# Two sets of projection tiles in plain fp32 instead of split products, and the scan's pace set by a count of the tiles' demands

## Chip, cores and metric

The kernel runs on 1 core of one Trainium2 chip. The metric is device time in microseconds from the start to the end of one execution. Before the change the median of 3 runs is 3599.55 us (3596.58 to 3600.33).

## What is computed

One sequence of 256 tokens of width 2048 runs through two blocks in fp32. The first (attention, a state-space branch and a large expert layer) isn't touched. The second, cut to what matters:

```python
h = rms_norm_2(x, norm_w[i])
proj = h @ w_in[i]
(g_qkv, g_z, g_b, g_a, r_feat, r_z, s_u, s_z, gate_logits) = _split_cols(proj, SPLIT_SIZES)
o_a = gdn_branch(g_qkv, g_z, g_b, g_a, ...)
o_b = rwkv7_branch(r_feat, r_z, ...)
o_c = s5_branch(s_u, s_z, ...)
gates = sigmoid(gate_logits + gate_b)          # 3 x 2048 columns
merged = sum(gates * einsum('blnc,ncd->blnd', stack([o_a, o_b, o_c]), w_branch), branch)
x = x + merged @ w_out
return rms_norm_2(x, final_norm_w)
```

S5 (`s5_branch`) is a complex diagonal recurrence over time on `s_u` (1024 channels, 32 groups of 128 states in the kernel). The recurrent branch (`rwkv7_branch`) takes keys and two small low-rank inputs out of `r_feat`.

## The kernel before, in words

**Tiles of weights.** Every projection streams weight tiles of 128 x 1024 fp32 (512 KB). The normal way (`wt`, L287) is in three terms: SyncE loads the tile into a `raw` buffer (L267, four buffers), ScalarE copies it to a reduced-precision high half `whi` (L281), VectorE subtracts to get the low half `wlo` (L285), and TensorE makes high x high, high x low and low x high (`mm3`, L298; lines 300 to 302). There are two `whi`/`wlo` pairs in the staging pool and a third in the second block (`self.third`), taken in turn. The other way (`whole`, L290) loads a tile straight into one of these `whi`/`wlo` buffers, seen as plain fp32, and needs no split; only the first block's output projection uses it (`tm_whole`, L1378, matmul at L1387, two times four groups of four tiles).

**Two shapes of projection.** `cm` (L1338) puts the weights' columns on the partitions: two tiles for 128 output columns, 8 contraction steps a tile, each of three products with 256 moving columns (L300 to L302), or two products (`mm2`, L304) where it is given room. `tm` (L1361) puts tokens on the partitions: eight tiles for 512 output columns, a tile having 2 contraction steps for each of 2 token halves, three products of 512 columns. Both are generators: a step loads and splits a tile (`yield`) and the next step issues its matmuls.

**The order of the work.** `feed` puts generators in one queue and `fill` (L1412) takes one step of the first. The second block's code calls `fill` between the instructions of its serial parts, so tiles lie between them. The tile framework then orders each engine's instructions by when they can run, with the order of the code as the priority; each engine works its own queue in order at run time.

**The second block's start.** `x2_stage` (L1289) ends the first block: it forms `x2` and `x1`, the norm's factors (L1311 to L1318), then `h3` (L1326) turns the normed state into `hT`, high and low halves of 16 chunks of 128 x 256: two TensorE turns a chunk (L443), a ScalarE copy (L453) and a VectorE subtraction (L455), both out of PSUM. Then VectorE rescales `x2` (L1322) and ScalarE's queue stores it to DRAM (`x3d`, L1323) for the residual. `block2` (L1464) allocates its pools over memory that `x1` and `x2` held. It feeds S5's inputs (`w2s`, 8 times `cm`, evacuated by `evu`), with the first three groups of gates after inputs 1, 2 and 3, then the keys (`w2rk`, 10 times `cm`, fed by `rwkv_front`, L1871, evacuated by `evk`), then four more gate groups; `gates` holds 12 groups in all. So 16 + 20 tiles of `cm` and 56 of `tm` lie in the queue when S5 starts.

**S5** (L1715) has 8 groups `j` of 4 state steps `i`. A group loads its tables (L1739, L1746), turns its input matrix (L1742) and copies it (L1744). A state step loads a cosine and sine table (L1751), TensorE makes the inputs (L1758, for two states at a time), VectorE multiplies twice (L1764, L1765), GpSimd combines (L1766, L1767), VectorE scans twice (L1770), GpSimd and VectorE multiply (L1771, L1772) and VectorE combines (L1773, L1774). `back` (L1729 to L1733) turns four states into outputs. After each state step `self.fill(3 if sc % 4 else 2)` takes 2 or 3 tiles from the queue. `self.until(("u", j))` takes tiles until input `j` is there.

`merged` (128 x 2 x 2048) collects the three branches, first written in the evacuation of `branch(2, ...)` long after S5.

Of the kernel before, what the change touches and what calls it, by code (L numbers as in the profile page):

```python
# [12 lines left out]
ALU = mybir.AluOpType  # L13
# [220 lines left out]
class K:  # L234
    def __init__(self, tc, A, at, dbg=None):
        self.tc, self.nc, self.A, self.at, self.dbg_ = tc, tc.nc, A, at, dbg
        self.n = 0
        self.pp, self.queue, self.done, self.bg = [], [], set(), []
        self.bgr, self.bgc = 1.0, 0.0
        self.side, self.later = [], [[] for _ in range(LAG)]  # L240
        self.nw = 0
        self.third, self.ns = None, 0
        self.more, self.nr = None, 0

    def t(self, pool, shape, dt=F32, tag=None, bufs=None):
        self.n += 1
# [23 lines left out]
    def split(self, src, n=1024, hi_e="act", lo_e="dve"):  # L270
        self.ns = (self.ns + 1) % 3
        p, tag, b = (self.third, "3", 1) if self.third and self.ns == 0 else (self.stg, "", 2)
        hi = self.t(p, [128, 1024], F32R, tag="whi" + tag, bufs=b)
        lo = self.t(p, [128, 1024], F32R, tag="wlo" + tag, bufs=b)
        self.hilo(hi[:, :n], lo[:, :n], src[:, :n], hi_e, lo_e)
        return hi, lo

    def hilo(self, hi, lo, src, hi_e="act", lo_e="dve"):
# [11 lines left out]
    def whole(self, src):  # L290

        self.nw = (self.nw + 1) % (6 if self.third else 4)
        p, n = (self.third, "3") if self.nw > 3 else (self.stg, "")
        t = self.t(p, [128, 1024], F32R, tag=("whi", "wlo")[self.nw % 2] + n, bufs=1 if n else 2).bitcast(F32)
        self.nc.sync.dma_start(t, src)
        return t

    def mm3(self, out, shi, slo, mhi, mlo, start, stop):  # L298
# [990 lines left out]
    def x2_stage(self, hp, xp, out, x1, nf, g2):  # L1289

        nc, tc = self.nc, self.tc
        V, ACT, PL = nc.vector, nc.scalar, nc.gpsimd
        scr = tc.alloc_tile_pool(name="scr2", bufs=1, space=DRAM)
        x3d = self.t(scr, [2, 128, D], tag="x3d")
        x2 = self.t(xp, [128, 2, D])
        ss = self.t(xp, [128, 2, 2, 4])
        for b in range(4):
            c = slice(b * 512, b * 512 + 512)
            for q in range(2):
                x, y = x2[:, q, c], x1[:, q, c]  # L1300
                V.tensor_tensor(x, out[4 * q + b], g2[:, c], op=ALU.mult)
                (PL if q and b < 2 else V).tensor_tensor(x, x, y, op=ALU.add)
                junk = self.t(xp, [128, 512], tag="junk", bufs=2)
                ACT.activation(junk, x, AF.Square, accum_out=ss[:, 0, q, b : b + 1])
                (V if q or b == 3 else PL).tensor_tensor(y, x, nf[:, c], op=ALU.mult)
                junk = self.t(xp, [128, 512], tag="junk", bufs=2)
# [12 lines left out]
        hT = self.h3(hp, xp, x1, v)  # L1319
        for q in range(2):  # L1320
            for c in (slice(0, 1024), slice(1024, 2048)):
                V.tensor_scalar(x2[:, q, c], x1[:, q, c], r[:, q : q + 1], None, op0=ALU.mult)  # L1322
            nc.scalar.dma_start(x3d[q], x2[:, q])  # L1323
        return hp, hT, x3d

    def h3(self, hp, pool, y, r):  # L1326

        hT = self.pair(hp, NK, "hh")
        hh, hl = hT[:2]
        dg = self.diag(pool, r, "dg3", 2)  # L1330
        n2 = self.cp("norm2", "cp3")
        for c in range(16):
            a = [y[:, q, c * 128 : c * 128 + 128] for q in range(2)]
            self.chunk_T(a, [dg[:, q] for q in range(2)], hh[:, c], hl[:, c], n2[:, c : c + 1], c % 2)
        return hT


    def cm(self, wd, j, hT, evac, key=None, nk=NK, room=None):  # L1338


        ps = self.t(self.acc, [128, 512], tag="acc")
        for half in range(2):
            hi, lo = self.wt(wd[2 * j + half], nk // 2 * 128)
            yield
            for k in range(nk // 2):
                kk = half * (nk // 2) + k
                sl = slice(k * 128, k * 128 + 128)
                if room:
                    self.mm2(ps, hi[:, sl], lo[:, sl], hT[2][:, kk], kk == 0, kk == nk - 1)
                else:  # L1350
                    self.mm3(ps[:, :S], hi[:, sl], lo[:, sl], hT[0][:, kk], hT[1][:, kk], kk == 0, kk == nk - 1)
        if room:
            s = room()
            self.nc.scalar.activation(s, ps[:, S:], AF.Copy)
            self.nc.vector.tensor_tensor(s, ps[:, :S], s, op=ALU.add)  # L1355
            evac(j, s)
        else:
            evac(j, ps[:, :S])
        self.done.add(key)

    def tm(self, wd, g, hT, evac, key=None, nk=NK):  # L1361
# [99 lines left out]
        self.flush()  # L1461


    def block2(self, hp, hT, x3d):  # L1464

        nc, tc, A = self.nc, self.tc, self.A
        V, ACT, PL = nc.vector, nc.scalar, nc.gpsimd
# [10 lines left out]
        merged = self.t(gt, [128, 2, D])  # L1478

        def gate(g):  # L1480
            def ev(g, q, ps):
# [10 lines left out]
        def branch(n, g4, o, last=None):  # L1492
            def ev(g, q, ps):
                c = slice(g4 * 512, g4 * 512 + 512)
                th = self.t(gt, [128, 512], tag="th", bufs=2)
                nc.sync.dma_start(th, gd[g, q])
                if n == 2:
                    V.scalar_tensor_tensor(merged[:, q, c], th, 1.0, ps, op0=ALU.add, op1=ALU.mult)
                else:
                    V.scalar_tensor_tensor(th, th, 1.0, ps, op0=ALU.add, op1=ALU.mult)  # L1500
                    (PL if last is None else V).tensor_tensor(merged[:, q, c], merged[:, q, c], th, op=ALU.add)
# [11 lines left out]
            ACT.activation(u[:, j], ps, AF.Copy)  # L1513

        gates = [gate(g) for g in (8, 9, 10, 11, 4, 5, 6, 7, 0, 1, 2, 3)]
        for j in range(8):
            self.feed(self.cm(A["w2s"], j, hT, evu, ("u", j)))
            if j in (1, 2, 3):
                self.feed(gates.pop(0))
        yT = out2("B")  # L1520
        kT = mB()
        self.rwkv_front(br, hT, kT)
        self.feed(*gates[:4])
        del gates[:4]
        self.s5(br, u, yT)
        oS = out2("A")
        gk, gq, gvz = self.gdn_front(br, hT)
# [17 lines left out]
        def last(g4):  # L1545
            for c in range(4 * g4, 4 * g4 + 4):
                ps = self.bank()
                for q in range(2):
                    nc.tensor.transpose(ps[:, q * 128 : q * 128 + 128], merged[:, q, c * 128 : c * 128 + 128], self.ident)
# [6 lines left out]
        self.dbg("merged", merged)  # L1556
        self.third = None
        gt.release()
        br.release()
        with tc.tile_pool(name="fin", bufs=1) as fp:  # L1560
            y = self.t(fp, [128, 2, D])
            fw = self.t(fp, [128, D])
# [152 lines left out]
    def s5(self, pl, u_, yT):  # L1715
# [7 lines left out]
        def back(j, u, cT, states):  # L1723
# [8 lines left out]
            ACT.activation(y, y, AF.Gelu_apprx_tanh)  # L1732
            self.hilo(yh[:, j], yl[:, j], y)  # L1733

        for j in range(8):
            self.until(("u", j))
            u = u_[:, j]
# [10 lines left out]
            for i in range(4):  # L1748
# [26 lines left out]
                states.append(a)  # L1775
                if late and i == 0:
                    late()
                self.fill(3 if sc % 4 else 2)
            late = partial(back, j, u, cT, states)
        late()  # L1780

# [86 lines left out]
            yield  # L1868


    def rwkv_front(self, pl, hT, kT):  # L1871
        nc, A = self.nc, self.A
        V, ACT, PL, mm = nc.vector, nc.scalar, nc.gpsimd, nc.tensor.matmul
        cp = lambda n: self.cp(n, "cp3")
# [44 lines left out]
                    nc.tensor.transpose(pt[:, q * 128 : q * 128 + 128], t[:, q * 128 : q * 128 + 128], self.ident)  # L1919
                V.tensor_copy(self.ba, pt[:, 0:256].rearrange("p (q c) -> p q c", q=2)[:, :, 96:112])  # L1920

        for j in range(10):
            self.feed(self.cm(A["w2rk"], j, hT, evk, ("rk", j)))
        self.rw = dict(shift=shift, wa=wa, half=half, oka=oka, ones=ones, hln=hln, pss=pss, kT=kT)

    def rwkv(self, pl, hT, out, extras):

# [360 lines left out]
    def run(self, upto=99, only=0):  # L2288
# [4 lines left out]
        if only == 2:  # L2293
# [7 lines left out]
            with tc.tile_pool(name="x3p", bufs=1) as p:  # L2301
# [6 lines left out]
                hT = self.h3(hp, p, x3, self.rstd(p, ss, 2, float(D)))  # L2308
            self.block2(hp, hT, x3d)
        else:  # L2310
            r = self.block1(upto)
            if r is not None:
# [26 lines left out]
```

## Time and profile before

| | |
|---|---|
| median of 3 runs | 3599.55 us |
| the profiled execution | 3600.31 us |
| its span, first to last instruction | 3598.2 us |
| mean granted TensorE clock | 0.979 |
| VectorE busy / ScalarE busy / GpSimd busy | 71% / 45% / 11% |

The profile is one execution, taken by the hardware profiler. Busy times are per engine. Matmuls are pipelined and their ends are modelled, so the busy time of a run of matmuls is not what they cost; the distance between starts is. PE is TensorE's matmuls, PEld its weight loads, DVE VectorE, ACT ScalarE, POOL GpSimd, SP SyncE. A granted clock of 1.00 is 2.4 GHz, 0.50 is 1.2 GHz.

### The profile page before, as it was taken

The page shows a single profiled execution, that of the slowest core. Times are in us where ns is not written, and L with a number is a line of the kernel's source. Part 1 is how long each engine was busy: PE and PEld are TensorE (multiplying, and loading weights), DVE is VectorE, ACT ScalarE, POOL GpSimd, SP SyncE. Part 2 cuts the span into 40 slices and gives each one's busy share as a digit, 9 for nine tenths or more (in the row PEclk, how much of TensorE's full clock was granted, in tenths as well). Part 3 has the DMA queues.
Part 4 walks back from the last instruction along what each step waited for, and adds up shares of the span by engine and source line. Part 5 has one row for each costly group of instructions (what it writes and reads, how often), then busy time and mean ns, then how long its engine had stood idle before and what let it go on. Part 6 is the DMA issues. An engine that isn't in the chain of part 4 may idle for free. (4 is left out here: it accounts for less than half of the span.)

```text
span 3598.2 us, 52389 instructions
## 1 busy us (share of the span) xinstructions
PE 3427.4 (95%) x18918; PEld 2852.2 (79%) x18918; DVE 2565.5 (71%) x4648; ACT 1632.8 (45%) x2934; POOL 390.3 (11%) x487
## 2 busy tenths in 40 slices
PE   5899999999999999999999998988999999999998
PEld 4888747888998888888878786776788888778887
DVE  7777666788887655565577658878777767666765
ACT  2355424444554444445555554333444444434444
POOL 0000010000000000000000002333223222021310
PEclk7999999999999999999999999999999999999999
DMA  9966785666456855566788765645533443434455
GB/s 345 333 222 206 266 290 177 199 198 201 159 162 208 257 185 186 187 203 205 240 271 287 254 206 186 203 160 180 169 113 113 150 138 108 134 123 159 146 182 186
DMA packets 237294, 710.40 MB, mean 197 GB/s; under 512 B 34091, under 2 KB 61804, under 8 KB 235756
## 3 DMA queue, kind: packets, MB, share of 16 engines
q1 hardware_dynamic: 207564, 672.08, 56.8%
q10 hardware_dynamic: 29472, 34.98, 2.9%
q8 instruction: 149, 2.44, 0.3%
q14 instruction: 109, 0.89, 0.1%
HBM read 673.87 MB, written 32.55 MB: 196 GB/s over the span
## 5 line engine op out<-in xcount | busy, mean ns | idle before, releaser
L285 DVE TENSOR_TENSOR wlo<-raw,whi 128x1024 fp32r<-128x1024 f32 (+1 forms) x951 | 1167.8, 1229 | 567.1 <-ACT whi L281 562.8
L281 ACT ACTIVATE whi<-raw 128x1024 fp32r<-128x1024 f32 (+1 forms) x951 | 994.0, 1046 | 1224.8 <-PE acc L302 577.3
L308 PE MATMUL acc<-hh,whi 128*128 128x512 f32 x3328 | 1197.9, 401 | 0.7 <-DVE cT L469 0.7
L309 PE MATMUL acc<-hh,wlo 128*128 128x256 f32 x3328 | 940.0, 282 | 7.1 <-DVE wlo L285 6.9
L308 PEld LDWEIGHTS acc<-hh,whi 128*128 128x128 f32 x3328 | 627.0, 188 | 145.6 <-issue 4.5
L309 PEld LDWEIGHTS acc<-hh,wlo 128*128 128x128 f32 x3328 | 629.6, 189 | 13.5 <-DVE wlo L285 12.0
L301 PE MATMUL acc<-wlo,wh 128*128 128x512 f32 x1024 | 402.1, 393 | 8.0 <-DVE wlo L285 7.2
L300 PE MATMUL acc<-whi,wh 128*128 128x512 f32 x1024 | 396.6, 390 | 3.5 <-DVE ge L1355 2.8
L302 PE MATMUL acc<-whi,wl 128*128 128x512 f32 x1024 | 399.3, 390 | 0.0
L301 PE MATMUL acc<-wlo,hh 128*128 128x512 f32 (+1 forms) x608 | 243.7, 401 | 14.9 <-DVE wlo L285 14.7
L300 PE MATMUL acc<-whi,hh 128*128 128x512 f32 (+1 forms) x608 | 248.1, 409 | 5.3 <-DVE r L1355 5.3
L302 PE MATMUL acc<-whi,hh 128*128 128x512 f32 (+1 forms) x608 | 242.1, 398 | 0.0
L301 PEld LDWEIGHTS acc<-wlo,wh 128*128 128x128 f32 x1024 | 192.5, 188 | 58.6 <-DVE wlo L285 18.8
L300 PEld LDWEIGHTS acc<-whi,wh 128*128 128x128 f32 x1024 | 192.3, 188 | 45.7 <-ACT wh L281 3.1
L302 PEld LDWEIGHTS acc<-whi,wl 128*128 128x128 f32 x1024 | 192.7, 188 | 38.9
L302 PE MATMUL acc<-hh,wlo 128*128 128x256 f32 x608 | 181.7, 299 | 27.9 <-DVE wlo L285 27.9
L300 PE MATMUL acc<-hh,whi 128*128 128x256 f32 x608 | 182.3, 300 | 5.4 <-ACT whi L281 3.4
L301 PE MATMUL acc<-hh,whi 128*128 128x256 f32 x608 | 178.5, 294 | 1.0 <-DVE hh L285 1.0
L301 PEld LDWEIGHTS acc<-wlo,hh 128*128 128x128 f32 x608 | 118.3, 195 | 43.1 <-DVE wlo L285 21.1
L302 PEld LDWEIGHTS acc<-hh,wlo 128*128 128x128 f32 x608 | 122.0, 201 | 34.0 <-DVE wlo L285 31.9
L1819 POOL TENSOR_TENSOR r<-r,cb 128x256 f32<-128x256 f32 x144 | 129.7, 920 | 163.7 <-DVE r L2149 38.1
L364 DVE SCALAR_TENSOR_TENSOR ada<-raw,u,ada 128x1024 f32<-128x1024 f32 x101 | 131.7, 1304 | 21.6 <-DMA raw<-in_ada_dram 20.7
(591 smaller groups left out, 4913.8 us busy)
## 6 DMA issues: line engine op xcount, KB each, us to landing
raw<-in_pu_dram SPq DMA_DIRECT2D x256, 512.0 KB, 3.6
raw<-in_pv_dram SPq DMA_DIRECT2D x252, 512.0 KB, 4.2
raw<-in_ada_dram SPq DMA_DIRECT2D x139, 512.0 KB, 5.2
raw<-in_w2gate_dram SPq DMA_DIRECT2D x96, 512.0 KB, 3.6
rawm<-in_ada_dram SPq DMA_DIRECT2D x53, 512.0 KB, 5.5
raw<-in_w2br_dram SPq DMA_DIRECT2D x48, 512.0 KB, 3.5
raw<-in_w2g_dram SPq DMA_DIRECT2D x48, 512.0 KB, 3.5
raw<-in_wq_dram SPq DMA_DIRECT2D x32, 512.0 KB, 3.6
```

What stands on the lines that cost most here:

```text
L281: nc.scalar.activation(hi, src, AF.Copy)
L285: self.lo = e.tensor_sub(lo, src, hi.bitcast(F32)).ins
L300: mm(out, shi, mhi, start=start, stop=False)
L301: mm(out, shi, mlo, start=False, stop=False)
L302: mm(out, slo, mhi, start=False, stop=stop)
L308: mm(out, hi, both, start=start, stop=False)
L309: mm(out[:, S:], lo, both[:, 0], start=False, stop=stop)
L364: nc.vector.scalar_tensor_tensor(acc, w, c, acc, op0=ALU.mult, op1=ALU.add)
L1819: PL.tensor_tensor(v2(lb), v2(L), cb(f"M{b}"), op=ALU.mult)
```

## The change

S5's inputs and the keys no longer use the split state `hT` and split weights but a whole fp32 state `hw` and whole tiles (`cm_whole`). `h3` first writes `hw` out of PSUM, by ScalarE and VectorE in turn, and then splits it into `hT`, two chunks at a time. `hw` lies in a pool `mg`, and `merged` takes over its buffer when it is first written. The rescale of `x2` is issued behind the last of these splits on VectorE. The queue becomes u0 u1 g u2 g u3 u4 g u5 u6 u7 g k0-2 g k3-5 g k6-9 g, with seven groups g of gates. `spare` adds 1 for a split tile and 2.2 for a whole one, is set to 0 once u0 is done, and each state step takes tiles until it reaches 4.2 a step. The squares' scratch in `x2_stage` uses two other buffers.

```diff
     def split(self, src, n=1024, hi_e="act", lo_e="dve"):
...
         self.hilo(hi[:, :n], lo[:, :n], src[:, :n], hi_e, lo_e)
+        self.spare += 1
         return hi, lo
...
         self.nc.sync.dma_start(t, src)
+        self.spare += 2.2
         return t
...
-        hT = self.h3(hp, xp, x1, v)
-        for q in range(2):
-            for c in (slice(0, 1024), slice(1024, 2048)):
-                V.tensor_scalar(x2[:, q, c], x1[:, q, c], r[:, q : q + 1], None, op0=ALU.mult)
-            nc.scalar.dma_start(x3d[q], x2[:, q])
-        return hp, hT, x3d
+        mgp = tc.alloc_tile_pool(name="mg", bufs=1)
+        hT, hw, last = self.h3(hp, mgp, xp, x1, v)
+        with tc.issue_after(last):
+            for q in range(2):
+                for c in (slice(0, 1024), slice(1024, 2048)):
+                    V.tensor_scalar(x2[:, q, c], x1[:, q, c], r[:, q : q + 1], None, op0=ALU.mult)
+                nc.scalar.dma_start(x3d[q], x2[:, q])
+        return hp, mgp, hT, hw, x3d
...
-        for c in range(16):
-            a = [y[:, q, c * 128 : c * 128 + 128] for q in range(2)]
-            self.chunk_T(a, [dg[:, q] for q in range(2)], hh[:, c], hl[:, c], n2[:, c : c + 1], c % 2)
-        return hT
+        for c in range(0, 16, 2):
+            ps = self.bank()
+            for i in range(2):
+                for q in range(2):
+                    self.turn(ps[:, i * S + q * 128 : i * S + q * 128 + 128], y[:, q, (c + i) * 128 : (c + i) * 128 + 128], dg[:, q])
+            nc.scalar.activation(hw[:, c], ps[:, :S], AF.Copy, scale=n2[:, c : c + 1])
+            nc.vector.tensor_scalar(hw[:, c + 1], ps[:, S:], n2[:, c + 1 : c + 2], None, op0=ALU.mult)
+        for c in range(0, 16, 2):
+            self.hilo(hT[0][:, c : c + 2], hT[1][:, c : c + 2], hw[:, c : c + 2])
+        return hT, hw, self.lo
...
+    def cm_whole(self, wd, j, h, evac, key=None):
+
+        ps = self.t(self.acc, [128, 512], tag="acc")
+        for half in range(2):
+            w = self.whole(wd[2 * j + half])
+            yield
+            for k in range(NK // 2):
+                kk = half * (NK // 2) + k
+                self.nc.tensor.matmul(ps[:, :S], w[:, k * 128 : k * 128 + 128], h[:, kk], start=kk == 0, stop=kk == NK - 1)
+        evac(j, ps[:, :S])
+        self.done.add(key)
...
-        for j in range(8):
-            self.feed(self.cm(A["w2s"], j, hT, evu, ("u", j)))
-            if j in (1, 2, 3):
-                self.feed(gates.pop(0))
+        us = [self.cm_whole(A["w2s"], j, hw, evu, ("u", j)) for j in range(8)]
         yT = out2("B")
         kT = mB()
-        self.rwkv_front(br, hT, kT)
-        self.feed(*gates[:4])
-        del gates[:4]
+        ks = self.rwkv_front(br, hw, kT)
+        gs, gates = gates[:7], gates[7:]
+        self.feed(us[0], us[1], gs[0], us[2], gs[1], us[3], us[4], gs[2], us[5], us[6], us[7], gs[3])
+        self.feed(*ks[:3], gs[4], *ks[3:6], gs[5], *ks[6:], gs[6])
         self.s5(br, u, yT)
...
+        self.until(("u", 0))
+        self.spare = 0.0
         for j in range(8):
...
-                self.fill(3 if sc % 4 else 2)
+
+                while self.spare < 4.2 * (sc + 1) and self.queue:
+                    self.fill()
...
-        for j in range(10):
-            self.feed(self.cm(A["w2rk"], j, hT, evk, ("rk", j)))
+        return [self.cm_whole(A["w2rk"], j, hw, evk, ("rk", j)) for j in range(10)]
```

## Rows read from the trace of the kernel before

**Rows 1.** The page, part 1: busy us, share of the span, instructions.
```profile
PE 3427.4 (95%) x18918; PEld 2852.2 (79%) x18918; DVE 2565.5 (71%) x4648; ACT 1632.8 (45%) x2934; POOL 390.3 (11%) x487
```
**Rows 2.** Busy time by window, the whole stage.
```profile
core 0: us, PE busy (x) PEld busy (x) DVE busy (x) ACT busy (x) POOL busy (x), PEclk, DMA share, GB/s
...
2193.50:2546.80 353.30, 314.46 (x1878) 256.69 (x1878) 297.95 (x425) 133.87 (x174) 120.81 (x111) 0.98 0.56 187
```
**Rows 3.** Busy time by window, two stretches of back-to-back split products.
```profile
2327.30:2338.50 11.20, 11.20 (x97) 11.13 (x93) 10.07 (x14) 4.67 (x8) 5.99 (x7) 1.00 0.53 183
2250.30:2261.20 10.90, 10.90 (x50) 8.85 (x48) 8.53 (x13) 4.83 (x6) 5.27 (x4) 1.00 0.69 242
```
**Rows 4.** Waits of TensorE in the stage: us in total, times, longest us.
```profile
PE acc L301 <- DVE wlo L285: 14.7, 12, 2.4
PE acc L302 <- DVE wlo L285: 13.6, 10, 2.3
PE sm L1758 <- DVE r L1744: 4.8, 5, 1.3
PE sm L1919 <- ACT r L1916: 3.7, 1, 3.7
```
**Rows 5.** Waits of VectorE in the stage.
```profile
DVE r L1770 <- POOL r L1766: 17.8, 27, 0.9
DVE r L1773 <- POOL r L1771: 12.6, 11, 1.2
```
**Rows 6.** Groups by line, VectorE, the stage: busy us, mean ns, idle before.
```profile
L285 DVE TENSOR_TENSOR wlo<-raw,whi 128x1024 fp32r<-128x1024 f32 x92 | 117.3, 1289 | 7.5 <-ACT whi L281 7.5
L1770 DVE TENSOR_TENSOR_SCAN r<-u,r 128x256 f32<-128x256 f32 x64 | 56.3, 919 | 17.8 <-POOL r L1766 17.8
L1772 DVE TENSOR_TENSOR r<-r,r 128x512 f32<-128x512 f32 x32 | 29.5, 922 | 0.8
...
L1765 DVE TENSOR_TENSOR r<-sm,r 128x512 f32<-128x512 f32 x32 | 21.7, 678 | 0.0
L1773 DVE TENSOR_TENSOR r<-r,r 128x256 f32<-128x256 f32 x32 | 13.4, 420 | 17.3 <-POOL r L1771 12.6 <-POOL r L1893 4.3
```
**Rows 7.** One line's instructions, L1766: duration ns min/median/max, first and last start.
```profile
L1766 POOL TENSOR_TENSOR r<-r,r x32: 727/746/1657, 2209.2 to 2530.5; 128x256 f32<-128x256 f32 x32
```
**Rows 8.** L1387, plain fp32: one of its four groups, and a window of it alone.
```profile
L1387 PE MATMUL acc<-wlo,hh x64: 592/592/697, 501.2 to 557.0; 128*128 128x512 f32 x64
...
522.90:547.00 24.10, 24.10 (x58) 10.64 (x56) 1.00 0.88 303
```
**Rows 9.** L1758, S5's input products: group in the stage, and eight on the timeline.
```profile
L1758 PE MATMUL sm<-mA,r 32*128 32x256 f32 x128 | 18.1, 400 | 4.8 <-DVE r L1744 4.8
...
2205.83 1.13 PE L1758 MATMUL sm<-mA,r 32*128 32x256 f32 x8
```
**Rows 10.** The state's preparation: groups by line, and two lines' instructions.
```profile
L453 ACT ACTIVATE hh<-sm,cp 128x256 fp32r<-128x256 f32 x16 | 7.0, 473 | 7.4 <-PE sm L443 7.3
...
L455 DVE SCALAR_TENSOR_TENSOR hh<-sm,cp,hh 128x256 fp32r<-128x256 f32 x16 | 7.1, 482 | 1.7 <-ACT hh L453 1.6
...
L1322 DVE TENSOR_SCALAR u<-u,rr 128x1024 f32<-128x1024 f32 x4 | 2.8, 749 | 0.9 <-POOL rr L325 0.9
...
L443 PE MATMUL sm<-dg,u x64: 271/275/554, 2189.4 to 2200.3; 128*128 128x128 f32 x64
```
**Rows 11.** DMA landings: the tensor x3d (last row of its view), and whole weight tiles.
```profile
DMA to landing us min/median/max: 3.6/4.3/5.6
...
whi<-in_wo_dram SPq DMA_DIRECT2D x16, 512.0 KB, 4.3
```
**Rows 12.** Timeline: S5's first load on SyncE, its first state's first instruction.
```profile
2200.66 0.33 SPq L1739 DMA_DIRECT2D r<-s5z  x1
...
2207.84 0.68 DVE L1764 TENSOR_TENSOR r<-sm,r 128x512 f32<-128x512 f32 x1
```
**Rows 13.** Busy time by window, an earlier stage (columns as rows 2).
```profile
600.00:800.00 200.00, 200.00 (x1161) 175.10 (x1160) 160.49 (x411) 93.21 (x139) 0.00 (x0) 1.00 0.63 198
```

More of the change, by code (lines that the diff above doesn't have):

```diff
@@ L1302, in x2_stage @@
                 (PL if q and b < 2 else V).tensor_tensor(x, x, y, op=ALU.add)
-                junk = self.t(xp, [128, 512], tag="junk", bufs=2)
+                junk = self.t(xp, [128, 1024], tag="adt", bufs=1)[:, :512]
                 ACT.activation(junk, x, AF.Square, accum_out=ss[:, 0, q, b : b + 1])
                 (V if q or b == 3 else PL).tensor_tensor(y, x, nf[:, c], op=ALU.mult)
-                junk = self.t(xp, [128, 512], tag="junk", bufs=2)
+                junk = self.t(xp, [128, 1024], tag="adr", bufs=1)[:, :512]
                 ACT.activation(junk, y, AF.Square, accum_out=ss[:, 1, q, b : b + 1])
@@ L1318, in x2_stage, with h3 @@
             r = self.rstd(xp, s[:, 0], 2, float(D))
-        hT = self.h3(hp, xp, x1, v)
-        for q in range(2):
-            for c in (slice(0, 1024), slice(1024, 2048)):
-                V.tensor_scalar(x2[:, q, c], x1[:, q, c], r[:, q : q + 1], None, op0=ALU.mult)
-            nc.scalar.dma_start(x3d[q], x2[:, q])
-        return hp, hT, x3d
-    def h3(self, hp, pool, y, r):
+        mgp = tc.alloc_tile_pool(name="mg", bufs=1)
[6 more added lines that the diff above has]
+        return hp, mgp, hT, hw, x3d
+    def h3(self, hp, mgp, pool, y, r):
+        nc = self.nc
         hT = self.pair(hp, NK, "hh")
-        hh, hl = hT[:2]
+        hw = self.t(mgp, [128, NK, S], tag="mg")
         dg = self.diag(pool, r, "dg3", 2)
         n2 = self.cp("norm2", "cp3")
-        for c in range(16):
-            a = [y[:, q, c * 128 : c * 128 + 128] for q in range(2)]
-            self.chunk_T(a, [dg[:, q] for q in range(2)], hh[:, c], hl[:, c], n2[:, c : c + 1], c % 2)
-        return hT
+        for c in range(0, 16, 2):
[8 more added lines that the diff above has]
+        return hT, hw, self.lo
     def cm(self, wd, j, hT, evac, key=None, nk=NK, room=None):
@@ L1461, in drain, with block2 @@
         self.flush()
-    def block2(self, hp, hT, x3d):
+    def block2(self, hp, mgp, hT, hw, x3d):
         nc, tc, A = self.nc, self.tc, self.A
@@ L1477, in block2, with merged @@
         gt = tc.alloc_tile_pool(name="gt", bufs=1)
-        merged = self.t(gt, [128, 2, D])
+        sums = []
+        def merged():
+            if not sums:
+                sums.append(self.t(mgp, [128, 2, D], tag="mg"))
+            return sums[0]
         def gate(g):
@@ L1496, in ev @@
                 nc.sync.dma_start(th, gd[g, q])
+                m = merged()[:, q, c]
                 if n == 2:
-                    V.scalar_tensor_tensor(merged[:, q, c], th, 1.0, ps, op0=ALU.add, op1=ALU.mult)
+                    V.scalar_tensor_tensor(m, th, 1.0, ps, op0=ALU.add, op1=ALU.mult)
                 else:
                     V.scalar_tensor_tensor(th, th, 1.0, ps, op0=ALU.add, op1=ALU.mult)
-                    (PL if last is None else V).tensor_tensor(merged[:, q, c], merged[:, q, c], th, op=ALU.add)
+                    (PL if last is None else V).tensor_tensor(m, m, th, op=ALU.add)
                 if last is not None and q == 1:
@@ L1548, in last @@
                 for q in range(2):
-                    nc.tensor.transpose(ps[:, q * 128 : q * 128 + 128], merged[:, q, c * 128 : c * 128 + 128], self.ident)
+                    nc.tensor.transpose(ps[:, q * 128 : q * 128 + 128], merged()[:, q, c * 128 : c * 128 + 128], self.ident)
                 ACT.activation(m_hh[:, c], ps[:, :S], AF.Copy, scale=0.5)
@@ L1555, in block2 @@
         self.drain()
-        self.dbg("merged", merged)
+        self.dbg("merged", merged())
         self.third = None
@@ L1559, in block2 @@
         br.release()
+        mgp.release()
         with tc.tile_pool(name="fin", bufs=1) as fp:
@@ L1733, in back @@
             self.hilo(yh[:, j], yl[:, j], y)
+        self.until(("u", 0))
+        self.spare = 0.0
         for j in range(8):
@@ L2307, in run @@
                     nc.scalar.activation(junk, x3[:, q], AF.Square, accum_out=ss[:, q : q + 1])
-                hT = self.h3(hp, p, x3, self.rstd(p, ss, 2, float(D)))
-            self.block2(hp, hT, x3d)
+                mgp = tc.alloc_tile_pool(name="mg", bufs=1)
+                hT, hw, _ = self.h3(hp, mgp, p, x3, self.rstd(p, ss, 2, float(D)))
+            self.block2(hp, mgp, hT, hw, x3d)
         else:
```

2 lines of the change are left out of this document (1 added, 1 removed).

## The prediction

> **What bounds the kernel now.** The page first: TensorE is busy for 95% of the span, VectorE for 71% [rows 1]. Then the stage that the diff touches, cut out by time, from the first S5 input matmul (2193.5 us) to the end of the gates' groups there (2546.8): 353.3 us, VectorE busy for 298.0 (84%), TensorE for 314.5 [rows 2]. That busy share is not TensorE at its peak. Back to back, 93 weight loads of 128x256 products take 11.2 us, 0.120 each, and 48 of 128x512 products 10.9 us, 0.227 each [rows 3]. The stage holds 56 gate tiles of 12 matmuls (2.72 us each, 152.5 in all) and 36 tiles of S5's inputs and the keys, of 24 (2.88, 103.7). With some 25 us of S5's own small matmuls that is 281; some 70 us are lost. The waits name VectorE: 14.7 us for the gates' low halves and 13.6 for those of the 36 tiles, then S5's own matmuls, 8.5 [rows 4]. VectorE itself waits only for GpSimd, in S5's state step: 17.8 and 12.6 us [rows 5]. Its account per state: (56.3+29.5+2x21.7+2x13.4)/32 = 4.88 us of the step, 2.9 low halves at 1.289 = 3.7, some 0.8 of evacuations (estimated from the 298 us), 1.0 of waiting: 10.4. The states run from 2209.2 to 2530.5, 31 intervals of 10.36 us [rows 6, 7]. So VectorE's queue sets today's pace, and TensorE (2.9 tiles, 8.0 us, and 0.8 of S5's own) waits.
>
> **The change, part by part.**
> *36 tiles go whole.* Each drops one split, 1.289 us of VectorE [rows 6]: 46.4 us. (ScalarE drops as many; it is no bound.) TensorE's side must be read with care. The kernel already has whole tiles (L1387): 128x512, plain fp32. Its 32 tiles of four products are 128 products, and the trace shows four groups of 64 records, so a product is two records. A record takes 24.1/56 = 0.430 us there, nothing idle [rows 8]; a product costs 0.86, against 3x0.227 = 0.68 in three terms. The same doubling stands in S5's own 64 input products, 128 records, of 256 columns: eight in 1.13 us, of which about 0.38 is the last one's latency, 0.107 each with two row groups side by side, so 0.215 [rows 9]. A whole tile is 8 products, 16 records: 3.44 us, instead of 2.88. Bounds for a record: 0.20 (the eight in 1.13 with a longer tail) and 0.43 (that of 512 columns); I take 0.215, which rows 8 and 9 both give. So TensorE gets 36x0.56 = **20 us more** work while VectorE gets 46 less.
> The rule that speaks against the change is in FP8 and Floating Point Precision of the Trainium skill, section TensorE Precision Notes: a true fp32 product is four passes through the array. The trace agrees: two records of two column times each. By a record for a product the tile would take 1.72 us; the rule lowers that rival's chance.
>
> *The state's preparation (h3).* Before: 16 ScalarE copies at 0.473 us and 16 VectorE subtractions at 0.482, chasing each other; the 64 transposing records run from 2189.4 to 2200.3 [rows 10]. After: eight evacuations on each engine, side by side, then eight splits of 512 columns on each (0.68 on VectorE, by the 512-column row L1765 [rows 6]): VectorE 9.3 instead of 7.7 us, +1.6. The transposes are then bound by themselves, 64 records of 128 columns at half of 0.215, 7 us, to about 2196.6, and S5's first tiles need no split: TensorE goes on at once.
>
> *The rescale of x2 moves behind the splits.* Four VectorE instructions of 0.749 us [rows 10]; behind them on ScalarE's queue the two x3d stores, landing 3.6 to 5.6 us after issue [rows 11]. ScalarE's first constants and high halves stand behind that, and S5's buffers, first loaded by SyncE at 2200.66, with the first state at 2207.84 [rows 12]. After: splits end near 2199, rescale near 2202, stores land near 2207.5, first state near 2212. Bounds: 0 and 9 us. Taken: 0, because TensorE has four whole tiles, 13.8 us, to about 2210; without that cover it would be the 9.
>
> *Whole loads wait on SyncE until TensorE frees a whi/wlo slot* (six, shared with the splits). Behind such a wait stand the gates' raw loads, S5's tables and the gate stores. Going through the turns of the slots, most whole loads get one last used three or more tiles back, 8 us for a landing of 4.3 [rows 11]; at the borders between groups a few (two, by my count) get the tile just before. Bounds 0 and 16 us; taken 3, since other ready work can go first.
>
> *The pace.* Before, 2 or 3 tiles a state. After, a state goes out when the tiles since the last one sum to 4.2, a gate tile counting 1, a whole one 2.2. Whole stretches, 1.91 tiles a state: TensorE 6.6+0.8+0.3 of S5's own work and waits = 7.7; VectorE 4.9+0.8+1.0 = 6.7. Gate stretches, 4.2 a state: TensorE 11.4+1.1 = 12.5; VectorE 6.7+5.4 = 12.1. TensorE becomes the longer one in both, barely in the second. Once three whole tiles are through, 33 are left: 17.3 states at 7.7 (133.2 us); the gates 13.3 at 12.5 (166.3). The last 1.4 states have no tiles and run beside the next stage, whose splits they delay: +3.
>
> *At nothing:* the order of the gates (the same 92 tiles, the stage's other work covers them); merged in another pool, whose first writer comes long after the keys; junk under other names (ScalarE writes it in its own order, behind VectorE's work).
>
> **Sum.** From 2196.6: three tiles 10.3, states 299.5, gates' waits for low halves as today 14.7, slots 3, last states 3: 2527.1, against 2546.8: -19.7; whole tiles and a VectorE that is no longer full leave the smaller gaps at most as they are. The profiled execution took 3600.3 us (span 3598.2), 0.8 over the median of the runs: 3580.6, **3581 us**. The stages behind are TensorE-bound and move forward as a block.
>
> **Rivals.**
> 1. *No change in the time.* TensorE's 20 us more eat what VectorE gives: of 70 us lost, only the 13.6 for the 36 tiles' halves and the shorter start (4) go: +20-18 = +2, 3602. For it: VectorE is still 12.1 of 12.5 us full in the gates' stretches. Against: where TensorE is the bound, VectorE may be 80% busy with no TensorE idle at all (600 to 800 us) [rows 13].
> 2. *Slower, by whole loads that come late.* If a load gets a slot only when the tile before it is done, a tile costs issue, landing and itself, 0.33+4.3+3.44 = 8.1 us. With one and a half tiles ahead it is 5.4: 36x1.9 = +70, 3650. It decides from where a tile costs above 4.0 us (36x0.55 = the 20), under two slots ahead. For it: after a gate group all slots were held by its splits, and SyncE works in order. Against: rows 8 ran with four slots at 303 GB/s, nothing idle.
> 3. *More gain, the gates' waits go.* VectorE gets ahead in the whole stretches, the 14.7 us of waits fall to 3: 3569.
> 4. *A record is a product.* Whole tiles at 1.72 us: TensorE -42, VectorE -45; the stage shrinks by some 42: 3559. Against: the count of rows 8 and 9.
> 5. *Slower, in the stretches of whole tiles:* states don't overlap and each is a chain of VectorE and GpSimd of some 8.5 us instead of 7.7: 17.3x0.8 = +14 on the forecast, 3595. That is no loss yet, but with rival 1 it is.
>
> **How the numbers follow.** About 0.2% (7 us) is what a measurement of this kernel tells from none. Forecast 0.46 (3572 to 3593); rival 3: 0.20; rival 4: 0.04; these three are faster: 0.70. Rival 1, with rival 5 as its neighbour: 0.18, nearly all of it within 0.2% (0.17), the rest slower. Rival 2: 0.12, slower, with 0.13 in all. Range for 8 in 10: down to 3562 (rival 3 without the slots' and last states' 6) and up to 3603 (rival 1); the late loads and rival 4 stay out.
>
> **What would show it.** Right: the stage is about 330 us long; whole products are two records 0.215 apart; 36 fewer 1024-wide L285; states about 7.7 us apart in the whole stretches and 12.5 to 13.5 in the gates'; VectorE below 80% of the stage; L302's waits for low halves gone. Wrong: whole tiles with TensorE idle before them, released by a DMA (rival 2); one record a product (rival 4); L301's waits for low halves above today's (rival 1); a first state past 2216 with TensorE idle before it.

## The result, and the profile after

The changed kernel takes 3642.18 us (median of four runs, 3635.24 to 3647.68) against 3599.94 before: ratio 1.0118, 95% interval 1.01 to 1.0135, slower by 42 us. The forecast was 3581. The profiled execution took 3647.68 us, 5.5 above its median.

The page's part 1 of the kernel after answers to [rows 1]: TensorE is busy as large a share of a longer span, VectorE 40 us less.

```profile
PE 3461.5 (95%) x18630; PEld 2869.9 (79%) x18630; DVE 2525.9 (69%) x4612; ACT 1597.8 (44%) x2898; POOL 376.7 (10%) x487
```

In all that follows the stage is cut from the first turning matmul of h3 to the first matmul of the stage behind it. Busy time by window of before, then of after (columns as in [rows 2]):

```profile
2189.40:2546.80 357.40, 318.16 (x1895) 260.10 (x1896) 301.09 (x430) 134.44 (x175) 121.50 (x112) 0.97 0.57 188
```
```profile
2192.70:2590.80 398.10, 347.79 (x1596) 271.34 (x1596) 253.04 (x377) 96.89 (x135) 104.79 (x106) 0.93 0.48 164
```

The stage grew by 40.7 us, out of the 47.7 by which the two profiled spans differ (3598.2 and 3645.9 us) and the 42 between the medians. VectorE fell from 301 to 253 us, as meant. TensorE's busy time rose by 29.6 us and its idle time, which was to shrink, rose from 39.2 to 50.3. What it waited for (TensorE's waits in the stage: us in total, times, longest us) is to be read against [rows 4]; the wait before L446, the first turn, lies ahead of the window:

```profile
PE acc L304 <- DVE wlo L287: 17.6, 8, 5.1
PE acc L1381 <- DMA cb<-in_cb_dram: 13.2, 1, 13.2
PE sm L446 <- issue: 6.3, 1, 6.3
PE acc L1381 <- DMA wlo<-in_w2s_dram: 5.7, 2, 3.5
PE acc L1381 <- DMA wlo<-in_w2rk_dram: 5.0, 2, 2.5
PE sm L1953 <- ACT r L1950: 4.6, 1, 4.6
PE sm L1790 <- DVE r L1776: 3.4, 2, 2.8
PE acc L1381 <- DMA whi<-in_w2rk_dram: 0.7, 1, 0.7
```

L304 is the gates' product with the low half (L301 before). The 13.6 us for low halves of the 36 tiles are gone. In their place the same tiles, now whole (L1381), wait 24.6 us for DMAs, and the gates' own low halves come later than before (17.6 instead of 14.7). The largest wait stands at the start; SyncE's waits there and the timeline show it whole:

```profile
SPq L297 <- DMA x3d<-u: 21.3, 2, 18.8
...
SPq L297 <- PE acc L305: 15.9, 9, 3.2
```
```profile
2201.33 3.62 PE L1381 MATMUL acc<-mg,wlo 128*128 128x256 f32 x16
...
2204.67 2.73 DVE L1327 TENSOR_SCALAR u<-u,rr 128x1024 f32<-128x1024 f32 x4
2206.12 1.66 ACTq L1328 DMA_DIRECT2D x3d<-u  x2
...
2212.60 0.33 SPq L297 DMA_DIRECT2D whi<-in_w2s_dram  x1
2212.61 0.36 ACTq L334 DMA_DIRECT2D cb<-in_cb_dram  x1
...
2212.98 0.42 SPq L297 DMA_DIRECT2D wlo<-in_w2s_dram  x1
2213.45 0.42 SPq L1771 DMA_DIRECT2D r<-s5z  x1
...
2218.13 3.33 PE L1381 MATMUL acc<-mg,whi 128*128 128x256 f32 x7 [13.18 <-DMA cb<-in_cb_dram]
```

One whole tile (16 records) runs at 2201.33. The load of the second is issued only at 2212.60: its slot is in the third split pair, in the pool that takes x2's memory, so it waits until the x3d stores (issued 2206.12) have read x2. The idle time is booked on the constants, but they were issued within 0.01 us of the tile's own load. S5's first load follows at 2213.45 (2200.66 before, [rows 12]).

A stall also leaves TensorE slow. Busy time by window, the stall and the stretch behind it:

```profile
2204.60:2218.10 13.50, 0.35 (x2) 0.00 (x0) 4.34 (x14) 1.49 (x2) 1.07 (x1) 0.67 0.71 272
2218.20:2234.00 15.80, 15.80 (x65) 12.89 (x66) 7.19 (x10) 2.66 (x4) 3.17 (x3) 0.85 0.19 71
```

In the second TensorE is never idle, and the granted clock averages 0.85; the seven records at 2218.13 stand some 0.42 us apart, twice the 0.216 of the same products when they run undisturbed (below), so they ran at the lower level, 1.2 GHz. Over the stage the granted clock is 0.93 against 0.97. The Trainium skill (TensorE: Matmul & The Clock Gate, HAM oscillation) says that waits for DMAs throttle the array, so that the work behind them starts cold; the trace agrees.

Low halves and states, answering to [rows 6, 7] (VectorE's groups; GpSimd's L1798, first and last start):

```profile
L287 DVE TENSOR_TENSOR wlo<-raw,whi 128x1024 fp32r<-128x1024 f32 x56 | 71.2, 1278 | 35.8 <-ACT whi L283 35.6
```
```profile
L1798 POOL TENSOR_TENSOR r<-r,r x32: 722/731/1649, 2227.7 to 2591.7; 128x256 f32<-128x256 f32 x32
```

36 fewer, exactly; but 31 intervals in 364.0 us are 11.7 us a state, where 10.36 were and 9.8 were forecast (10.3 with the waits for low halves).

### The profile page after: what moved, and what is told of

Read it like the earlier page. It is cut to its first block, busy times and chain, and to the rows that moved or that the text cites. A ratio compares the mean times of both kernels' runs of the same rounds, so it can differ in the third digit from the quotient of the medians.

```text
span 3645.9 us, 51669 instructions
## 1 busy us (share of the span) xinstructions
PE 3461.5 (95%) x18630; PEld 2869.9 (79%) x18630; DVE 2525.9 (69%) x4612; ACT 1597.8 (44%) x2898; POOL 376.7 (10%) x487
## 5 line engine op out<-in xcount | busy, mean ns | idle before, releaser
L287 DVE TENSOR_TENSOR wlo<-raw,whi 128x1024 fp32r<-128x1024 f32 (+1 forms) x915 | 1121.0, 1226 | 589.5 <-ACT whi L283 582.7
L283 ACT ACTIVATE whi<-raw 128x1024 fp32r<-128x1024 f32 (+1 forms) x915 | 956.3, 1046 | 1170.1 <-PE acc L305 559.8
L312 PE MATMUL acc<-hh,wlo 128*128 128x256 f32 x3328 | 940.0, 283 | 8.0 <-DVE wlo L287 8.0
L312 PEld LDWEIGHTS acc<-hh,wlo 128*128 128x128 f32 x3328 | 629.5, 189 | 14.7 <-DVE wlo L287 12.9
L304 PE MATMUL acc<-wlo,wh 128*128 128x512 f32 x1024 | 403.1, 394 | 7.6 <-DVE wlo L287 6.8
L304 PE MATMUL acc<-wlo,hh 128*128 128x512 f32 (+1 forms) x608 | 242.3, 398 | 17.6 <-DVE wlo L287 17.6
L304 PEld LDWEIGHTS acc<-wlo,wh 128*128 128x128 f32 x1024 | 193.0, 188 | 58.9 <-DVE wlo L287 19.1
L304 PEld LDWEIGHTS acc<-wlo,hh 128*128 128x128 f32 x608 | 118.0, 194 | 43.4 <-DVE wlo L287 21.0
L303 PEld LDWEIGHTS acc<-whi,hh 128*128 128x128 f32 x608 | 118.0, 194 | 34.7 <-issue 11.5
L305 PEld LDWEIGHTS acc<-whi,hh 128*128 128x128 f32 x608 | 117.7, 194 | 24.8 <-issue 0.3
L1187 ACT ACTIVATE ge<-ge 128x256 f32<-128x256 f32 x128 | 53.4, 417 | 149.2 <-DVE ge L1367 149.2
L305 PE MATMUL acc<-hh,wlo 128*128 128x256 f32 x320 | 100.4, 314 | 11.5 <-DVE wlo L287 11.4
```

The lines of the kernel that those rows point to most:

```text
L283: nc.scalar.activation(hi, src, AF.Copy)
L287: self.lo = e.tensor_sub(lo, src, hi.bitcast(F32)).ins
L303: mm(out, shi, mhi, start=start, stop=False)
L304: mm(out, shi, mlo, start=False, stop=False)
L305: mm(out, slo, mhi, start=False, stop=stop)
L312: mm(out[:, S:], lo, both[:, 0], start=False, stop=stop)
```

## The experiments

My theory behind the result: the loss is in the slots that the whole tiles share with the splits, at the start and all along; the new order and plain fp32 by themselves are harmless or good. Rivals: the late rescale, the order and pace, plain fp32's price. Every kernel computes the whole reference. All are edits of the kernel after. Times are medians; a ratio is to the kernel before, with its 95% interval.

**One cure at a time.**

The first four whole tiles in the staging pairs:
```diff
-        self.third, self.ns = br, 0
+        self.third, self.ns, self.nw = br, 0, 5
```


> The changed kernel with the turn of whole tiles through the slots begun so that its first four tiles fall into the staging pool and not, as the second and third now do, into the third pair, which lies over memory that x2's store still reads. Theory (the start): the 13.4 us in which TensorE stands behind the second whole tile go, and with them half-clock time behind; the constants and S5's buffers still wait for the store, so 10 to 18 us come back: 3624 to 3632. Rival (something else holds the second tile, or the gates' splits stand behind the store and take the wait over): under 4 us, 3638 or more.

The rescale of x2 and its stores ahead of h3:
```diff
+        for q in range(2):
+            for c in (slice(0, 1024), slice(1024, 2048)):
+                V.tensor_scalar(x2[:, q, c], x1[:, q, c], r[:, q : q + 1], None, op0=ALU.mult)
+            nc.scalar.dma_start(x3d[q], x2[:, q])
         hT, hw, last = self.h3(hp, mgp, xp, x1, v)
-        with tc.issue_after(last):
...
```


> The changed kernel with the rescale of x2 and its stores issued ahead of the state's preparation instead of behind its splits. Theory (the start): the stores land some 10 us earlier, before the second whole tile is wanted, and all that waits for them (whole tiles in the third pair, constants, S5's first tables) goes earlier; against that 2.8 us of VectorE stand in front of the preparation: 8 to 15 us come back, 3627 to 3634. Rival (the start costs nothing that isn't caught up later, as S5's pace sets the end): under 4 us.

S5's inputs and keys split again, all else as after:
```diff
-        us = [self.cm_whole(A["w2s"], j, hw, evu, ("u", j)) for j in range(8)]
+        us = [self.cm(A["w2s"], j, hT, evu, ("u", j)) for j in range(8)]
...
-                while self.spare < 4.2 * (sc + 1) and self.queue:
+                while self.spare < 2.8 * (sc + 1) and self.queue:
```


> The changed kernel with S5's inputs and the keys in three split products again (24 matmuls a tile instead of 16 records), all else of the change kept: order of the gates, preparation, rescale behind the splits, states paced by the count of tiles at 2.8. Theory (plain fp32 itself costs 20 us of TensorE and pays nothing back): the late start, now of splits that wait for the state's halves, stays, the stage loses TensorE's 20 us and the whole tiles' late loads (11 us): 3605 to 3622. Rival (VectorE's 46 us saved were worth it, and the loss is order, start and pace): with the splits back it gets slower or stays, 3640 or more.

Whole tiles loaded into the four buffers of the raw tiles, so that no whole tile holds a split's slot (these four are shared too, with the loads of the tiles that are split):
```diff
-            w = self.whole(wd[2 * j + half])
+            w = self.t(self.stg, [128, 1024], tag="raw", bufs=4)
+            self.nc.sync.dma_start(w, wd[2 * j + half])
+            self.spare += 2.2
```


> The changed kernel with whole tiles loaded into the four raw buffers instead of the split pairs' slots. Theory (whole loads come late because a slot is freed by the tile just before): TensorE's waits for whole loads (11.4 us after the start) shrink or go, and the second tile no longer lies over x2's memory, so the start's 13.4 us go as well: 15 to 25 us come back, 3617 to 3627. Rival (raw buffers held until TensorE is done keep the gates' loads back instead): the waits move to the gates' low halves, and no more than the start's 10 to 13 us come back, 3629 or more.

Measured: rotation 3633.48 (1.0092, 1.0057 to 1.0126), 1.5 us above its forecast; rescale 3628.12 (1.0077, 1.0054 to 1.0101), as forecast; split 3610.82 (1.0038, 1.0019 to 1.0056), as forecast; raw buffers **3599.32** (1.0004, 0.9989 to 1.0019), a miss, 18 us better than I gave it. The start alone is 9 to 14 us of the loss, the slots together 43. With raw buffers, the stage's window, TensorE's waits, the timeline at the start and the states read so (of the waits, L446's lies ahead of the window and L1761's behind it):

```profile
2185.90:2540.40 354.50, 333.55 (x1597) 263.60 (x1597) 251.72 (x378) 98.89 (x136) 109.97 (x106) 0.97 0.56 188
```
```profile
PE acc L304 <- DVE wlo L287: 10.8, 8, 2.8
PE sm L446 <- issue: 6.4, 1, 6.4
PE sm L1955 <- ACT r L1952: 4.1, 1, 4.1
PE sm L1761 <- DVE r L1807: 3.8, 1, 3.8
PE sm L1792 <- DVE r L1778: 3.5, 2, 1.9
PE sm L1776 <- DMA r<-s5z: 2.5, 2, 1.8
```
```profile
2194.85 13.98 PE L1383 MATMUL acc<-mg,raw 128*128 128x256 f32 x64
```
```profile
L1800 POOL TENSOR_TENSOR r<-r,r x32: 722/732/1655, 2215.3 to 2541.2; 128x256 f32<-128x256 f32 x32
```

No whole tile waits for a DMA, the gates' low halves come earlier than in either kernel, four whole tiles run back to back at the start (the cover that the forecast counted on), and the clock is back at 0.97. The same records (1597, 1596) are busy for 333.6 us instead of 347.8: of the 43.6 us by which the stage is shorter, 14.2 are busy time on the same records (the clock was 0.93 in the one and 0.97 in the other), 29.4 idle time. The clock is not one execution's chance: over the whole execution it reads 0.971 to 0.978 in the four runs of the change and 0.977 to 0.985 in the ten with raw buffers.

**What was left: start, order, pace.** Raw buffers with the rescale moved as well; raw buffers with pace 4.0; the split version with the rescale moved; raw buffers with the order and the pace of before:
```diff
-        self.feed(us[0], us[1], gs[0], us[2], gs[1], us[3], us[4], gs[2], us[5], us[6], us[7], gs[3])
-        self.feed(*ks[:3], gs[4], *ks[3:6], gs[5], *ks[6:], gs[6])
+        self.feed(us[0], us[1], gs[0], us[2], gs[1], us[3], gs[2], *us[4:])
+        self.feed(*ks, *gs[3:])
...
-                while self.spare < 4.2 * (sc + 1) and self.queue:
-                    self.fill()
+                self.fill(3 if sc % 4 else 2)
```


> The whole tiles in the buffers of raw tiles, and besides x2's rescale and its stores ahead of h3. Slots theory (the late rescale hurts only because the second and third whole tiles' slots lie over x2): with raw buffers nothing at the start waits for the stores but S5's first loads, which are covered by four whole tiles (14.0 us, 2194.8 to 2208.8), so moving the rescale costs its 2.7 us ahead of the turns and gives nothing back: 3599 to 3604. Rival (S5's late start costs by itself, since its chain is the last to end): the chain starts some 3 us earlier and the stage ends earlier: 3593 to 3597.

> The whole tiles in the buffers of raw tiles, and the pace 4.0 in place of 4.2 per state. Pace theory (S5's last state is issued with the queue empty; its way out then makes TensorE wait 4.2 us behind the stage, at 2547): a faster pace ends the chain some 5% of 134 units earlier, so this wait goes and 2 to 4 us come: 3595 to 3598. Rival (the states then ask VectorE for more than it has beside the gates' splits, and the low halves come later by as much): 3599 to 3604.

> S5's inputs and the keys split again, in the order and at the even pace of after, with x2's rescale ahead of h3. Start theory (what the split version in the new order lost against before, 11 to 13 us, is the 19.0 us that TensorE waited for S5's first input behind the late stores): it goes, less 2.7 us of rescale ahead: 3595 to 3601, so order and pace alone are worth nothing. Rival (the order and the even pace cost by themselves): 3605 to 3612.

> The whole tiles in the buffers of raw tiles, but the order of the tiles and the pace of before (all of S5's inputs with three gates behind j 1, 2, 3, then all the keys, then four gates; 3 tiles a state, 2 at each fourth). This is plain fp32 by itself with buffers that hold no split. If the order and the pace are what lets VectorE's saving be used: the last four gates keep VectorE full as in before (a state's 7 us and three splits against three gate tiles of 5.5 us), TensorE adds its 21 us in the stretch of whole tiles: 3606 to 3620. If only the buffers mattered: within 3 us of the version with the new order, 3597 to 3602.

Measured: raw and rescale **3594.84** (0.9983, 0.9971 to 0.9996); pace 4.0 3606.03 (1.002, 1.001 to 1.003); split and rescale 3601.68 (1.0011, 1.0001 to 1.0021); old order 3606.17 (1.0014, 0.9998 to 1.0029).

The split version wins 9 us from the rescale and ends 0.7 us above its theory's range: with its start cured, order, pace and the new preparation together are worth nothing to tiles that are split (3601.7 against 3600.0). The wait that went, TensorE's for S5's first input, in the split version with the late rescale and then with the early one:

```profile
PE sm L1774 <- DMA r<-s5z: 19.0, 3, 11.5
```
```profile
PE sm L1773 <- DMA r<-s5z: 7.6, 2, 3.8
```

For whole tiles the new order and pace together look worth 7 us (3606.2 to 3599.3), but the two ratios' intervals overlap, so it is not shown. My reading, argued only: the order puts whole and gate tiles side by side, so VectorE's saving falls where its load is. The rescale ahead of h3 gained 4.5 us by the medians (these intervals overlap too) where the slots theory gave nothing; its rival (S5's chain is late by itself) was nearer. The faster pace lost 7 us, 2 more than its rival gave, and not by the rival's way: the low halves came no later (10.5 us of waits against 10.8), while TensorE's waits for S5's own products went up (L1792: 8.8 us against 3.5).

**How much to make whole, and what the splits lack.** On raw and rescale: pace 4.4; only the keys whole, pace 3.6; only S5's inputs whole, pace 3.45 (as the split version, for one family); and all whole, but splits in S5's stage without the third pair:
```diff
-        p, tag, b = (self.third, "3", 1) if self.third and self.ns == 0 else (self.stg, "", 2)
+        p, tag, b = (self.third, "3", 1) if self.third and self.ns == 0 and not self.two else (self.stg, "", 2)
...
+        self.two = True
         self.s5(br, u, yT)
+        self.two = False
```


> Raw buffers for the whole tiles, the rescale ahead of h3, and the pace 4.4 in place of 4.2 (4.0 cost 7 us). If a pace that asks less of VectorE per tile leaves fewer waits for the gates' low halves (12.1 us with 4.2): 3590 to 3594. If the last states, now some 3 with no tiles left, cost as much behind the stage: 3595 to 3602.

> The same, with the keys' 20 tiles whole and S5's 16 input tiles split as before; the pace 3.6, so that the states still end with the tiles. TensorE gets 9.3 us less work than with all 36 whole (16 tiles of 3.48 against 2.88 us), VectorE 16 low halves of 1.29 more, 20.6. If VectorE's relief is already enough with 20 whole tiles: 3586 to 3591. If every low half taken back shows up as a wait of TensorE: 3595 to 3606.

> The mirror: S5's 16 input tiles whole, the keys' 20 split; the pace 3.45. TensorE gets 12 us less work than with all 36 whole, VectorE 25.8 us more. Same reading: 3584 to 3590 if VectorE has room, 3595 to 3608 if it has none.

> Raw buffers, the rescale ahead of h3, all 36 whole, but S5's stage splits only into two of the three pairs: it takes away what the whole tiles took from the splits, and nothing else. If what cost after some 30 us behind its start is that the splits lack pairs: 3610 to 3625. If it is the whole loads themselves, which wait on SyncE for a pair that TensorE still reads: 3595 to 3602.

Measured: pace 4.4 3606.04 (1.0021, 1.0007 to 1.0036); keys whole 3598.50 (1.0004, 0.9992 to 1.0015); inputs whole 3609.56 (1.0023, 1.0008 to 1.0038); two pairs 3621.66 (1.0053, 1.0032 to 1.0073). Pace 4.4 missed both of its readings, inputs whole lies 1.6 us above its second; keys whole is in its second, two pairs in its first. Both neighbours of pace 4.2 are slower, by 7 us (intervals that overlap) and by 11; why 4.2 stands out was not found. With one family whole the time is 4 and 15 us above that with both; since the pace had to differ too, and pace alone moves as much, this settles little. Without the third pair 27 us are lost though no whole tile holds a pair's slot. Windows of the stage and waits in it, TensorE's and ScalarE's, first with three pairs (raw and rescale), then with two:

```profile
2176.10:2528.30 352.20, 332.81 (x1596) 263.59 (x1597) 253.99 (x378) 98.75 (x136) 110.10 (x106) 0.97 0.56 189
```
```profile
PE acc L304 <- DVE wlo L287: 12.1, 8, 2.8
...
ACT whi L283 <- PE acc L305: 67.8, 34, 6.3
```
```profile
2193.30:2570.10 376.80, 339.01 (x1596) 265.71 (x1597) 254.90 (x382) 98.91 (x136) 110.24 (x108) 0.96 0.53 178
```
```profile
PE acc L304 <- DVE wlo L287: 26.9, 14, 3.9
...
ACT whi L283 <- PE acc L305: 91.6, 38, 8.2
```

VectorE's busy time is the same (254.0, 254.9). It has the time for the splits, but no place to put them ahead of need: ScalarE, which writes the high halves first, waits 91.6 us in place of 67.8 for TensorE to be done with a gate tile, and TensorE waits 14.8 us more for low halves. Its idle time in the stage rises by 18.4 us, its busy time by 6.2.

**Two open points.** The evacuation of a whole tile behind the next tile's split in place of ahead of it; and the change with both cures of its start, slots shared as it has them:
```diff
-        evac(j, ps[:, :S])
-        self.done.add(key)
+        self.defer.append(lambda: (evac(j, ps[:, :S]), self.done.add(key)))
...
+            while self.defer:
+                self.defer.pop(0)()
             for f in late[0]:
```


> Raw buffers, rescale ahead of h3, pace 4.2, and a whole tile's evacuation is issued behind the next tile's load and split in place of ahead of them. If the low halves that TensorE still waits for (12.1 us, eight times, most at the first gate tile behind whole ones) are late because the high half stands on ScalarE behind an evacuation that itself waits for the whole tile: those waits fall to 4 to 8 us and the time to 3588 to 3592. If they are late because the low half stands on VectorE behind a state's steps and its waits for GpSimd: the waits stay at 10 to 14 us and the time at 3594 to 3599.

> The change with its slots shared as it has them, but with both cures of the start: the first four whole tiles in the staging pairs, and the rescale ahead of h3. What is left above the version with raw buffers (3595) is then the sharing behind the start. If splits that lack a pair are all of it (taking the third pair away cost 27 us): 3612 to 3622. If the start still held a part that either cure alone left (TensorE waited 6.2 us for S5's whole tiles with the rescale moved, 14.8 for the keys' with the rotation): 3604 to 3611.

Measured: later evacuation 3596.04 (0.9992, 0.998 to 1.0004), low halves' waits 15.0 us, not lower: it is not ScalarE's order that delays them. The other reading, VectorE's queue, can be seen in the trace of raw and rescale: each of the eight low halves that TensorE waited for stands right behind a state's steps, and in five of the eight (9.0 of the 12.1 us) VectorE had just idled 1.2 us for GpSimd. The longest (L1806 and L1807 end a state's steps):

```profile
2300.65 0.43 DVE L1806 TENSOR_TENSOR r<-r,r 128x256 f32<-128x256 f32 x1 [1.16 <-POOL r L1804]
2300.99 0.42 DVE L1807 TENSOR_TENSOR r<-r,r 128x256 f32<-128x256 f32 x1
2301.33 1.22 DVE L287 TENSOR_TENSOR wlo<-raw,whi 128x1024 fp32r<-128x1024 f32 x1
...
2302.60 0.50 PE L304 MATMUL acc<-wlo,hh 128*128 128x512 f32 x1 [2.76 <-DVE wlo L287]
```

No run took S5's steps away. Both cures: 3631.23 (1.0093, 1.007 to 1.0116), a miss for both readings; two cures are no better than one. The rotation moves a late load elsewhere (it is there with the rotation alone too, 11.4 us). In the timeline of the version with both:

```profile
2496.64 0.33 SPq L297 DMA_DIRECT2D wlo<-in_w2rk_dram  x1
...
2501.50 1.28 DVE L1515 TENSOR_TENSOR th<-acc,gb 128x512 f32<-128x512 f32 x2
...
2502.22 1.23 ACT L1516 ACTIVATE th<-th 128x512 f32<-128x512 f32 x2 [11.22 <-DVE th L1515]
...
2502.88 0.92 SPq L1517 DMA_DIRECT2D gd<-th  x2
2503.89 0.41 SPq L297 DMA_DIRECT2D whi<-in_w2rk_dram  x1
...
2509.43 2.07 PE L1380 MATMUL acc<-mg,whi 128*128 128x256 f32 x4 [11.53 <-DMA whi<-in_w2rk_dram]
...
2514.79 3.62 PE L1380 MATMUL acc<-mg,wlo 128*128 128x256 f32 x16
```

The whole load stands on SyncE behind a gate's store, the store behind ScalarE's tanh, the tanh behind a VectorE add, and the add behind S5's steps in VectorE's queue. TensorE waits 11.5 us for the end of that chain, though SyncE had issued four other whole loads from 2491.15 to 2496.64: the tile that TensorE runs next, at 2514.79, is one of them, but these tiles come later in TensorE's order. So sharing has two prices behind the start: splits without a pair and whole loads that come late in SyncE's order. Their shares of the 33 us between the rescale alone (3628.1) and the rescale with raw buffers (3594.8) were not separated; the missing pair can give up to the 27 it cost alone.

## Why the prediction was wrong

**The step that failed: "Whole loads wait on SyncE until TensorE frees a whi/wlo slot ... Bounds 0 and 16 us; taken 3".** It priced only the whole tile's own landing, and only at two borders. The sharing cost some 43 us. Against the version with raw buffers, TensorE waited 24.6 us for whole loads where it waited for none, 6.8 us more for the gates' low halves (17.6 against 10.8), whose splits lost pairs, and was busy 14 us longer with the same records at a lower clock. (27 us is what a third pair costs when it is taken away by itself; it overlaps with these and does not add to them.) The bound above, 16, was too low by a factor near three, because three things were not in it: the load over x2's memory, the way back from whole tiles to the splits, and the slower clock.

**The rescale, "taken 0, because TensorE has four whole tiles, 13.8 us".** The cover was not there: the second and the third of the four had slots over x2, which the rescale's stores keep. The condition ("without that cover it would be the 9") was right; the stall was 13.2 us, and the cure gave 14. The forecast went through the turns of the slots but not through where the third pair's memory lies.

**The loss that could go.** "Some 70 us are lost" was measured against records back to back; only 38.8 of them (353.3 less 314.5) were idle time, the rest TensorE's busy time above that rate. In the raw buffers whole tiles bring the stage's idle time from 39.2 down to 20.9 us (minus 18) and its busy time up by 15.4, where 20 was forecast, so of the rest about 5 came back (an estimate): the stage is 2.9 us shorter, not 19.7, and its states are 10.5 us apart (325.9 us for 31), not 9.8. The sum's 299.5 us for the states took every matmul at the back-to-back rate. Idle time down by 18 against more work is rival 1's working (+20-18, 3602), and the version with raw buffers is at 3599.3. That the two 18s agree is in part luck: 13.6 of the 18 went as that rival had it, but the rest came mostly from the gates' low halves (14.7 to 10.8) and not from the start. A slip besides: 3600.3 less 19.7 forecasts the profiled execution; the median would be 3579.9, not 3581.

**Right.** The record: four whole tiles, 64 records, in 13.98 us, 0.216 apart, 3.45 a tile (3.44 forecast). The rule on fp32 products in the Trainium skill (FP8 and Floating Point Precision, TensorE Precision Notes) holds here, two records of two column times. VectorE: 36 splits fewer, 48 us less busy (46.4 less 1.6 forecast). The turns took 8.5 us (7 forecast, 10.9 before).

**The rivals.** Rival 2 (slower by late whole loads, 3650, chance 0.12) came nearest to 3642, though not by every tile costing 5.4 us: by one stall of 13 us, smaller waits, and splits that lost their place. Three of the four signs named for a wrong forecast are in the profile: whole tiles idle before, released by DMAs; the gates' waits above 14.7; a first state past 2216 (its products run at 2225) with TensorE idle before it.

The best version, raw buffers and the early rescale, is 0.17% faster than before (0.9983, 0.9971 to 0.9996); its near twin with the later evacuation reads 0.9992, so the gain is small at best. In the same order and with the same start, plain fp32 in the raw buffers is worth 7 us against the split version (3601.7 to 3594.8; the intervals do not overlap): about a third of the 19.7 that were forecast.

## What to carry to other kernels

Before an operand moves from one kind of buffer to another, count who else uses the slots: a load that needs a slot which the other kind frees late takes lead from both, and an engine with time to spare cannot use it without a place to write ahead. Sharing as such is not the price: the four raw buffers were shared as well, and there no whole tile waited. Ask of each early buffer what lay in its memory before, and who still reads that. Separate a bottleneck's lost time into idle and slow before counting on it: here relieving VectorE gave back 18 us of the 39 idle ones and about 5 of the slow ones.

## What the runs showed of the hardware that was not expected

Waits can cost twice on TensorE. For the same 1596 records the stage's busy time goes from 332.8 us (idle 19.4, granted clock 0.97) over 339.0 (idle 37.8, 0.96) to 347.8 (idle 50.3, 0.93): in these three versions 31 us of idle time came with 15 us of slower work. It is no fixed rate, as two other versions show: the rescale alone, and the split version with the early rescale.

```profile
2188.50:2570.90 382.40, 345.77 (x1596) 270.91 (x1596) 252.96 (x377) 96.52 (x135) 105.45 (x106) 0.94 0.50 171
```
```profile
2192.70:2554.80 362.10, 326.74 (x1894) 264.34 (x1894) 303.67 (x420) 132.14 (x170) 119.74 (x112) 0.94 0.54 184
```

The first idles 36.6 us, less than with two pairs, and is busy 6.8 us longer. The second idles 35.4 us, less than the kernel before (39.2), and is busy 8.6 us longer with the same records (0.94 against 0.97). How much idle time there is does not tell the price; what else does was not found. Behind the stall of 13.5 us records ran 0.42 us apart instead of 0.216, at the lower clock level, with TensorE never idle.
